# A feed-forward stage with seven forms: x split a second time with the norm's factor in it, and the forms further apart

## The chip, the cores and the metric

The kernel runs on one core of a Trainium2 chip. The core has TensorE (PE in the profile; PEld is its loading of weights), VectorE (DVE), ScalarE (ACT), GpSimd (POOL) and SyncE (SP), which only issues transfers. Each engine takes its own queue of instructions in order; semaphores tie the queues together. The metric is the device time of one execution in microseconds, as the median of several runs.

## The reference

The reference is a decoder trunk of two layers on 256 tokens of 1024 features in float32. Each layer is feed-forward, mixer, feed-forward. All that the change touches is in the feed-forward stages:

```python
def rms_norm(x, g):
    xf = x.astype(jnp.float32)
    y = xf * lax.rsqrt(jnp.mean(xf * xf, axis=-1, keepdims=True) + EPS)
    return (y * g.astype(jnp.float32)).astype(x.dtype)

def swiglu(h, w_gate_up, w_down):
    a, b = jnp.split(h @ w_gate_up, 2, axis=-1)
    return (jax.nn.silu(a) * b) @ w_down

    x = x + 0.5 * swiglu(rms_norm(x, ffn1_norm), ffn1_w_gate_up, ffn1_w_down)
    ...
    x = x + 0.5 * swiglu(rms_norm(x, ffn2_norm), ffn2_w_gate_up, ffn2_w_down)
```

The hidden width is 2816, that is 22 groups of 128 columns for `a` and as many for `b`. The norm multiplies each token by a factor r (one number per token) and each feature by a gain g.

## The kernel before

**Split operands.** Every float32 operand is split into a high part that TensorE reads exactly in its fast float32 form and a low remainder: ScalarE copies (`hi`, L174 or L163), VectorE subtracts (`lo`, L175 or L164). A product is then hi times (hi and lo of x, 512 columns) plus lo times hi of x (256 columns).

**Units.** The weights come in units of 1 MB (128 x 2048). `fetch` loads the next unit of a list (`plan`) from SP's queue into one of four `raw` buffers and splits it in two halves of 128 x 1024 each; the split parts have room for three units (six half tiles each of `hi` and `lo`). `unit` hands the next split unit to TensorE. One unit is fetched ahead of the one in use.

**A feed-forward stage** (`ffn`). x lies with features on the partitions. `split_x` makes the eight tiles of `hx` (high and low part, x times gain g) at the end of the stage before. The upward half makes for each of the 22 groups n a "pair": 32 products over the eight tiles of hx into a bank of PSUM for a and b together. `drain` brings it to the tile `ab` (ScalarE copies one part, L223, VectorE adds the other, L224). `post(n)` follows one pair later: VectorE multiplies `ab` by r (L393), ScalarE takes Silu (L395), VectorE multiplies by b (L396), and `halves` splits the result for the downward half (L246, L247). r itself is made by `sums` during the first two pairs (`factor_spread`, L345 to L360): two products by ones, then five VectorE and ScalarE steps, of which L359 is the last.

**The seven forms.** In three of the four feed-forward stages (all but the very first), four groups, n = 12 to 15, are not made as pairs. Their 512 columns of a and b, for 256 tokens and 1024 features, form a block product of two by two blocks, which is made with seven products of half the size instead of eight (Strassen's and Winograd's scheme). Each form has 16 products into a bank with tokens on the partitions (`by_tokens`, names pa, pe, pg, pf in the trace) and needs a unit of weights of its own: the forms "1", "2" and "4" read parts of hx, the forms "5", "3", "6", "7" read sums of quarters of x (`x_forms`, made from `xg` = x times gain in the buffer `pre`, then split into tiles `sf`). The weights of "1", "5", "6" and "4" lie one after the other in one buffer (`sa`), each made by an accumulating transfer onto the one before (L155, issued by GpSimd, since it adds in flight); "3" and "7" share the buffer `pre` in the same way; "2" has a `raw` buffer. A form's transfer can go out only when the form before it in the same buffer is split. The results are added and subtracted in VectorE (L506 to L514), gated with Silu (`gated`, L471 to L477) and turned back to features by four transposes (`turned`). Since r is a factor per token, and tokens are on the partitions there, `gated` scales by a column of per-token factors, which `factor_tokens` makes with two more small products (st in the trace).

**Banks.** "1" and "2" accumulate in bank a, "5" and "3" in e, "6" has g, "7" is the first in f and "4" writes f again, anew, after "7" was read.

**Order.** TensorE's instructions keep the written order. The other engines' queues are ordered at build time by a planner: of what is ready by its own cost estimates it takes what was written first; `behind` adds an edge that holds one instruction back until another one of the same engine. The written order of the stage is 0, 1, 2, 3, 4, "1", 5, "2", 6, "5", 7, "3", 8, "6", 9, "7", 10, "4", 11, 16, ... 21 (`feed_order`).

Of the kernel before, what the change touches and what calls it, by code (L numbers as in the profile page):

```python
# [18 lines left out]
F32 = mybir.dt.float32  # L19
F32R = mybir.dt.float32r  # L20
# [34 lines left out]
def feed_order():  # L55

    z, forms = [], list(FORMS)
    for n in (*range(GROUP), *range(GROUP + 4, NF)):
        if n >= FIRST and forms:
            z.append(forms.pop(0))  # L60
        z.append(n)
    return z


def feed_units(base):
    return [base + n if isinstance(n, int) else (base, n) for n in feed_order()]

# [5 lines left out]
def trunk_kernel(ctx: ExitStack, tc: tile.TileContext, x_in, w_in, pw_in, qkn_in, rope_in, mask_in, band_in, out):  # L73
# [37 lines left out]
    for base in (0, FU, LU, LU + FU):  # L111
        plan.extend(feed_units(base) if base else range(NF))
# [13 lines left out]
    def fetch(last=None):  # L126

        u = next(plan)
        if isinstance(u, tuple):
            ahead.append(sum_form(*u))  # L130
            return
        raw, hi, lo = buffers()
        n = HALF if u < 4 else 2 * HALF
        for c in range(0, 2 * HALF, n):
            nc.sync.dma_start(raw[:, c:c + n], w_in[u, :, c:c + n])
# [4 lines left out]
        ahead.append((hi, lo))  # L140

    sums_at = {}

    def sum_form(base, f):

        n = base + GROUP
        q = {"11": (n, 0), "12": (n + 2, 0), "21": (n, 1), "22": (n + 2, 1)}
        at, add, src = FORMS[f]
        if at == "c":
            sums_at["c"] = raws.tile([P, 2 * HALF], F32, name="raw", tag="raw")  # L150
        z = sums_at[at].rearrange("p (i c) -> p i c", i=2)
        u, kh = q[src]
        w = w_in[u:u + 2, :, kh * HALF:(kh + 1) * HALF].rearrange("u p c -> p u c")
        if add:
            nc.gpsimd.dma_start(z, w, accum_op=OP.add)  # L155
        else:
            nc.sync.dma_start(z, w)
        _, hi, lo = buffers(False)
        z = z.rearrange("p i (k c) -> p i k c", c=2 * P)
        for h in range(2):  # L160
            a = z[:, :, 2 * h:2 * h + 2, :]
            hv, lv = (t[h].rearrange("p (k i c) -> p i k c", i=2, c=2 * P) for t in (hi, lo))
            act(hv, a, AF.Copy)  # L163
            tt(lv, a, hv.bitcast(F32), op=OP.subtract)  # L164
        return hi, lo

    def buffers(raw=True):
        raw = raws.tile([P, 2 * HALF], F32, name="raw", tag="raw") if raw else None
        hi = [parts.tile([P, HALF], F32R, name="hi", tag="hi") for _ in range(2)]
        lo = [parts.tile([P, HALF], F32R, name="lo", tag="lo") for _ in range(2)]  # L170
        return raw, hi, lo

# [160 lines left out]

    def factor_tokens():

        st = quarter("st")[:, 0, :2]
        for t in range(2):
            mm(st[:, t:t + 1], lhsT=acc[:, t * P:(t + 1) * P], rhs=ones[:, :1], start=True, stop=True)
        rt = small.tile([P, 2], F32, name="rt", tag="rt", bufs=2)
        rsqrt(rt, st, 1.0 / D)  # L340
        nt = small.tile([P, 2], F32, name="nt", tag="nt", bufs=1)
        nc.vector.tensor_scalar(nt, rt, -1.0, None, op0=OP.mult)
        return rt, nt

    def factor_spread():  # L345
# [19 lines left out]
    def ffn(after, n0=0, end=False, col=None):  # L365
        gs, gt = [], []

        def room(n, m):
            g = acts.tile([P, m, 2, S], F32R, name=n, tag=n)
            gt.append(g)  # L370
            gs.extend(g[:, i] for i in range(m))

        room("ga", 8)
        room("gc", 4)
        abs_ = {}

# [9 lines left out]
        def sums():  # L386
            r.append(factor_spread())
            if not n0:
                r.append(factor_tokens())

        def post(n):
            ab = abs_[n]
            scaled = tt(ab, ab, bc2(r[0]), op=OP.mult)  # L393
            sg = small.tile([P, S], F32, name="sg", tag="sg", bufs=2)
            act(sg, ab[:, 0, :], AF.Silu)  # L395
            tt(sg, sg, ab[:, 1, :], op=OP.mult)  # L396
            halves(gs[n], sg)
            return scaled

        if n0:  # L400
            room("gd", 4)
            room("gb", NF - 16)
            ws = [unit() for _ in range(n0)]
# [14 lines left out]
        else:  # L418
# [7 lines left out]
            drain(wide(1), pss[1])  # L426

            sums_at["a"] = acts.tile([P, 2 * HALF], F32, name="sa", tag="gd")
            pre = acts.tile([P, 12 * S], F32, name="pre", tag="gb")
            sums_at["b"] = pre[:, :NK * S]  # L430
            xg = pre[:, :NK * S].rearrange("p (k s) -> p k s", s=S)
            vt = acts.tile([P, 2, GW], F32, name="vt", tag="v")
# [3 lines left out]
            sf = {}  # L436

            def x_forms():

                late = drained[-1]  # L440
                for k in range(NK):
                    behind(act(xg[:, k, :], x[:, k, :], AF.Copy, scale=gain[:, l_of[0], col + k:col + k + 1]), late)  # L442
                a11, a21 = (xg[:, :4, t * P:(t + 1) * P] for t in range(2))
                a12, a22 = (xg[:, 4:, t * P:(t + 1) * P] for t in range(2))
# [26 lines left out]
            def gated(c, t, n, sign):  # L471

                c = c.rearrange("p (i j s) -> p i j s", i=2, j=2)
                sc = r[1][sign][:, t:t + 1]
                sg = small.tile([P, S], F32, name="sg", tag="sg", bufs=2)
                act(by_half(sg), c[:, :, 0, :], AF.Silu, scale=sc)
                stt(by_half(gq[2 * t + n]), c[:, :, 1, :], sc, by_half(sg), op0=OP.mult, op1=OP.mult)  # L477

            def turned(n):

                pt = quarter("pt")
                for i in range(2):
                    for t in range(2):
                        keep(nc.tensor.transpose(pt[:, i, t * P:(t + 1) * P], gq[2 * t + n][:, i * P:(i + 1) * P], ident))
                g = gt[2][:, 2 * n:2 + 2 * n]
                act(g[:, :, 0, :], pt, AF.Copy)
                tt(g[:, :, 1, :], pt, g[:, :, 0, :].bitcast(F32), op=OP.subtract)
# [3 lines left out]
            def strassen(f):  # L491
# [9 lines left out]
                elif f == "2":  # L501
                    gated(z, 0, 0, 0)
                elif f == "5":
                    act(p5, z, AF.Copy)
                elif f == "6":
                    tt(p1, z, p1, op=OP.add)  # L506
                    tt(c12, bank["e"], p1, op=OP.add)
                    gated(c12, 0, 1, 1)
                elif f == "7":
                    tt(p5, z, p5, op=OP.add)  # L510
                    tt(p5, p5, p1, op=OP.add)
                    gated(p5, 1, 1, 1)
                elif f == "4":
                    tt(p1, z, p1, op=OP.add)  # L514
                    gated(p1, 1, 0, 0)

            late = []
            wait = [0, 1]
            for i, n in enumerate(feed_order()[2:]):
                if isinstance(n, str):  # L520
                    strassen(n)
                    if n in "74":
                        late.append([2, 1 if n == "7" else 0])
                    continue
                pair(unit(), wide(n))
                fetch()
                if i == 0:
# [4 lines left out]
                if n == GROUP - 1:  # L532
                    room("gd", 4)
                    room("gb", NF - 16)
                for z in late:
# [3 lines left out]
            for m in wait:  # L539
                post(m)  # L540
        for b in range(NK * NF):
# [476 lines left out]
```

## Time and profile before

| what | value |
|---|---|
| three runs | 1009.3, 1012.51, 1013.52 us |
| median | 1012.51 us |
| the profiled execution | 1010.54 us, its span 1008.8 us |
| TensorE busy | 997.2 us |
| VectorE busy | 808.9 us |
| ScalarE busy | 641.5 us |
| mean granted clock of TensorE | 0.998 of full |

The span is the time from the first to the last instruction of the program; the time of an execution has a little around it. A row of the time line gives start, duration, engine, line, operation, out<-in, shapes, and in brackets the idle time of the engine before it with what ended it. Consecutive instructions of one engine overlap by a little, so the distance between starts tells what one costs in a full queue.

### The profile page before, as it was taken

To read this page: it belongs to the slowest core of one execution; us is meant where nothing else is said; L and a number is where in the kernel's file an instruction comes from. 1 tells how busy PE (TensorE), PEld (TensorE's weight loads), DVE (VectorE), ACT (ScalarE), POOL (GpSimd) and SP (SyncE) were. 2 spreads that over 40 slices of the span, in tenths; PEclk is the share of its full clock that TensorE was granted. 3 is DMA by queue.
4 is the path that set the end of the run, shared out by engine and by line. 5 is a ranking of instruction groups with operands and counts; after the bars stand their busy time and mean duration, and the time that the engine had idled before them with its cause. 6 is when DMAs were issued, how large, how long until landed. Compare 5 with 4: busy or idle time off the path is not lost.

```text
span 1008.8 us, 16140 instructions
## 1 busy us (share of the span) xinstructions
PE 997.2 (99%) x6336; PEld 904.4 (90%) x6336; DVE 808.9 (80%) x1217; ACT 641.5 (64%) x1026; POOL 30.6 (3%) x58
## 2 busy tenths in 40 slices
PE   9999999999999999999999999999999999999998
PEld 8988988898899988889998888988989999889888
DVE  6998866698978897986679798666988888889852
ACT  7866655657756876665578576555677568666641
POOL 0000000002000010000000000000020000000000
PEclk9999999999999999999999999999999999999999
DMA  8855655644537488565558856555544464967540
GB/s 301 309 203 209 209 195 187 213 167 150 188 136 262 162 243 238 201 215 183 195 209 235 229 204 229 193 204 183 184 182 173 142 245 161 261 195 250 205 151 21
DMA packets 34156, 202.34 MB, mean 201 GB/s; under 512 B 3488, under 2 KB 4768, under 8 KB 13088
## 3 DMA queue, kind: packets, MB, share of 16 engines
q1 hardware_dynamic: 30816, 188.74, 52.6%
q0 software_dynamic: 3264, 12.58, 6.8%
q8 instruction: 49, 0.80, 0.3%
q14 instruction: 27, 0.22, 0.1%
HBM read 200.26 MB, written 1.05 MB: 200 GB/s over the span
## 4 chain that ended last, share of the span: by engine, by line
PE 81%; DMA 9%; DVE 4%; ACT 3%; issue 2%; SPq 0%; ACTq 0%; POOLq 0%
PE ps L103 65%; DMA sa<-w 7%; PE pt L103 7%; PE two L103 4%; DVE lo L164 1%; DMA pre<-w 1%; PE pe L103 1%; DVE lo L175 1%; PE pf L103 1%; PE sc L103 1%; ACT hi L163 1%; ACT pre L442 1%; PE pt L657 1%; DVE ab L224 1%; PE y L103 1%
## 5 line engine op out<-in xcount | busy, mean ns | idle before, releaser
L103 PE MATMUL ps<-hx,hi 128*128 128x512 f32 x1504 | 506.9, 384 | 0.9 <-ACT hi L174 0.9
L175 DVE TENSOR_TENSOR lo<-raw,hi 128x1024 fp32r<-128x1024 f32 (+2 forms) x348 | 411.1, 1189 | 111.5 <-ACT hi L174 109.2
L174 ACT ACTIVATE hi<-raw 128x1024 fp32r<-128x1024 f32 (+2 forms) x348 | 352.8, 1026 | 180.0 <-PE ps L103 128.5
L103 PE MATMUL ps<-hx,lo 128*128 128x256 f32 x1504 | 411.0, 273 | 0.0
L103 PEld LDWEIGHTS ps<-hx,hi 128*128 128x128 f32 x1504 | 282.4, 188 | 51.8 <-ACT hi L174 1.2
L103 PEld LDWEIGHTS ps<-hx,lo 128*128 128x128 f32 x1504 | 282.6, 188 | 0.3 <-DVE lo L175 0.3
L103 PE MATMUL ps<-ga,hi 128*128 128x512 f32 (+1 forms) x264 | 87.0, 376 | 0.0
L103 PE MATMUL ps<-ga,lo 128*128 128x256 f32 x256 | 69.9, 273 | 0.0
L103 PE MATMUL ps<-gb,hi 128*128 128x512 f32 (+1 forms) x198 | 65.6, 376 | 0.0
L103 PE MATMUL pt<-hi,hx 128*128 128x512 f32 x192 | 65.1, 385 | 0.0
L103 PEld LDWEIGHTS ps<-ga,hi 128*128 128x128 f32 x264 | 49.0, 188 | 8.3
L103 PE MATMUL pt<-lo,hx 128*128 128x256 f32 x192 | 52.6, 274 | 0.0
L393 DVE TENSOR_TENSOR ab<-ab,r 128x512 f32<-128x512 f32 x76 | 51.9, 685 | 0.9
L103 PE MATMUL ps<-gb,lo 128*128 128x256 f32 x192 | 52.4, 273 | 0.0
L224 DVE TENSOR_TENSOR ab<-ps,ab 128x512 f32<-128x512 f32 x74 | 50.6, 684 | 0.9
L395 ACT ACTIVATE sg<-ab 128x256 f32<-128x256 f32 x76 | 31.3, 415 | 30.4 <-DVE ab L393 29.3
L103 PEld LDWEIGHTS ps<-ga,lo 128*128 128x128 f32 x256 | 48.1, 188 | 0.0
L163 ACT ACTIVATE hi<-sa 128x1024 fp32r<-128x1024 f32 x24 | 25.3, 1052 | 30.3 <-DMA sa<-w 26.9
L103 PE MATMUL ps<-gc,hi 128*128 128x512 f32 (+1 forms) x132 | 44.3, 376 | 0.0
L103 PE MATMUL ps<-gd,hi 128*128 128x512 f32 (+1 forms) x132 | 44.3, 376 | 0.0
L103 PE MATMUL ps<-mk,hi 128*128 128x256 f32 x256 | 44.1, 275 | 0.0
L223 ACT ACTIVATE ab<-ps 128x512 f32<-128x512 f32 x74 | 42.9, 579 | 0.0
(215 smaller groups left out, 1463.9 us busy)
## 6 DMA issues: line engine op xcount, KB each, us to landing
raw<-w SPq DMA_DIRECT2D x167, 1024.0 KB, 4.9
sa<-w POOLq DMA_DIRECT2D x9, 1024.0 KB, 10.0
raw<-w SPq DMA_DIRECT2D x16, 256.0 KB, 5.3
sa<-w SPq DMA_DIRECT2D x3, 1024.0 KB, 5.8
pre<-w SPq DMA_DIRECT2D x3, 1024.0 KB, 5.1
pre<-w POOLq DMA_DIRECT2D x3, 1024.0 KB, 13.0
out_dram<-gx SPq DMA_DIRECT2D x8, 128.0 KB, 2.6
gx<-x SPq DMA_DIRECT2D x3, 256.0 KB, 5.4
```

What stands on the lines that cost most here:

```text
L103: return keep(nc.tensor.matmul(*args, **kw))
L163: act(hv, a, AF.Copy)
L164: tt(lv, a, hv.bitcast(F32), op=OP.subtract)
L174: act(hi, w, AF.Copy)
L175: return tt(lo, w, hi.bitcast(F32), op=OP.subtract)
L223: act(t, ps[:, :, 1, :], AF.Copy)
L224: drained.append(tt(t, ps[:, :, 0, :], t, op=OP.add))
L393: scaled = tt(ab, ab, bc2(r[0]), op=OP.mult)
L395: act(sg, ab[:, 0, :], AF.Silu)
L442: behind(act(xg[:, k, :], x[:, k, :], AF.Copy, scale=gain[:, l_of[0], col + k:col + k + 1]), late)
L657: keep(nc.tensor.transpose(pt[:, h, o * P:(o + 1) * P], pr[:, h, c * P:(c + 1) * P], ident))
```

## The change

Five things change, all in the three stages with forms, beside a tidier `buffers`:

1. After pair 2, `scaled_x` makes `xs` = x times gain times r, eight steps of VectorE (128 x 256), where `xg` was made without r by eight ScalarE copies. After pair 3, `split_again` splits `xs` into `hx` once more, over the old values: four ScalarE copies and four VectorE subtractions of 128 x 512. All pairs from 4 on, and all forms, then have r in their products.
2. So `post` multiplies by r only for the groups 0 to 3, `gated` scales by 1 or -1, and `factor_tokens` goes.
3. `x_forms` moves from behind pair 2 to behind pair 4, its first sums held back until pair 4 is drained.
4. The order is written out: 0 to 5, "1", 6, "2", 7, "5", 8, "3", 9, 10, "7", 11, 16, "6", 17, 18, "4", 19, 20, 21. "7" comes before "6"; the sums for the last quarter move from "7" to "6" accordingly, and both `turned` come after "4".
5. The first loads of the two buffers ("1" and "3") are issued by GpSimd instead of SP.

```diff
-FIRST = 5
+FEED = (0, 1, 2, 3, 4, 5, "1", 6, "2", 7, "5", 8, "3", 9, 10, "7", 11, 16, "6", 17, 18, "4", 19, 20, 21)
...
         if add:
             nc.gpsimd.dma_start(z, w, accum_op=OP.add)
+        elif at == "c":
+            nc.sync.dma_start(z, w)
         else:
-            nc.sync.dma_start(z, w)
+            nc.gpsimd.dma_start(z, w)
...
         def sums():
             r.append(factor_spread())
-            if not n0:
-                r.append(factor_tokens())
...
-        def post(n):
+        def post(n, scale=True):
             ab = abs_[n]
-            scaled = tt(ab, ab, bc2(r[0]), op=OP.mult)
+            scaled = tt(ab, ab, bc2(r[0]), op=OP.mult) if scale else None
...
+            def scaled_x():
+
+                for k in range(NK):
+                    c = gain[:, l_of[0], col + k:col + k + 1]
+                    stt(xs[:, k, :], x[:, k, :], c, r[0], op0=OP.mult, op1=OP.mult)
+
+            def split_again():
+
+                for k in range(0, NK, 2):
+                    act(hx[:, k:k + 2, 0, :], xs[:, k:k + 2, :], AF.Copy)
+                    tt(hx[:, k:k + 2, 1, :], xs[:, k:k + 2, :], hx[:, k:k + 2, 0, :].bitcast(F32), op=OP.subtract)
...
             def x_forms():
 
-                late = drained[-1]
-                for k in range(NK):
-                    behind(act(xg[:, k, :], x[:, k, :], AF.Copy, scale=gain[:, l_of[0], col + k:col + k + 1]), late)
...
-                tt(s1, a22, a21, op=OP.subtract)
+                behind(tt(s1, a22, a21, op=OP.subtract), last)
+                behind(tt(s3, a11, a21, op=OP.subtract), last)
                 stt(s2, s1, -1.0, a11, op0=OP.mult, op1=OP.subtract)
-                tt(s3, a11, a21, op=OP.subtract)
...
                 elif f == "6":
                     tt(p1, z, p1, op=OP.add)
+                    tt(p5, p5, p1, op=OP.add)
+                    gated(p5, 1, 1, -1.0)
                     tt(c12, bank["e"], p1, op=OP.add)
-                    gated(c12, 0, 1, 1)
+                    gated(c12, 0, 1, -1.0)
                 elif f == "7":
                     tt(p5, z, p5, op=OP.add)
-                    tt(p5, p5, p1, op=OP.add)
-                    gated(p5, 1, 1, 1)
...
-            for i, n in enumerate(feed_order()[2:]):
+            for i, n in enumerate(FEED[2:]):
                 if isinstance(n, str):
                     strassen(n)
-                    if n in "74":
-                        late.append([2, 1 if n == "7" else 0])
+                    if n == "4":
+                        late += [[1, 1], [2, 0]]
                     continue
                 pair(unit(), wide(n))
                 fetch()
-                if i == 0:
+                if n == 2:
+                    scaled_x()
+                if n == 3:
+                    split_again()
+                if n == 4:
                     x_forms()
                 for m in wait[:2]:
-                    post(m)
+                    post(m, m < 4)
...
             for m in wait:
-                post(m)
+                post(m, False)
```

More of the change, by code (lines that the diff above doesn't have):

```diff
@@ L52 @@
 }
[L55 to L66, printed above, removed]
 C_G1, C_GM, C_G2, C_BG, C_PS, NG = 0, 8, 16, 24, 40, 44
@@ L111, in trunk_kernel @@
     for base in (0, FU, LU, LU + FU):
-        plan.extend(feed_units(base) if base else range(NF))
+        plan.extend([base + n if isinstance(n, int) else (base, n) for n in FEED] if base else range(NF))
         plan.extend(range(base + NF, base + NF + NF // 2))
@@ L132, in fetch @@
         raw, hi, lo = buffers()
-        n = HALF if u < 4 else 2 * HALF
-        for c in range(0, 2 * HALF, n):
-            nc.sync.dma_start(raw[:, c:c + n], w_in[u, :, c:c + n])
+        nc.sync.dma_start(raw, w_in[u])
         for h in range(2):
@@ L140, in fetch, with buffers, part_buffers @@
         ahead.append((hi, lo))
+    def buffers():
+        raw = raws.tile([P, 2 * HALF], F32, name="raw", tag="raw")
+        return raw, *part_buffers()
+    def part_buffers():
+        return [[parts.tile([P, HALF], F32R, name=n, tag=n) for _ in range(2)] for n in ("hi", "lo")]
     sums_at = {}
@@ L165, in sum_form @@
         return hi, lo
[L167 to L171, printed above, removed]
     def split(w, hi, lo):
@@ L332, in spread @@
         return r
[L334 to L343, printed above, removed]
     def factor_spread():
@@ L365, in ffn, with room @@
     def ffn(after, n0=0, end=False, col=None):
[L366 to L374, printed above, removed]
+        gs, gt = {}, {}
+        def room(name, n0, m):
+            g = acts.tile([P, m, 2, S], F32R, name=name, tag=name)
+            gt[name] = g
+            gs.update({n0 + i: g[:, i] for i in range(m)})
+        room("ga", 0, 8)
+        room("gc", 8, 4)
         abs_ = {}
@@ L400, in ffn @@
         if n0:
-            room("gd", 4)
-            room("gb", NF - 16)
+            room("gd", 12, 4)
+            room("gb", 16, NF - 16)
             ws = [unit() for _ in range(n0)]
@@ L426, in ffn @@
             drain(wide(1), pss[1])
+            pre = acts.tile([P, 12 * S], F32, name="pre", tag="gb")
             sums_at["a"] = acts.tile([P, 2 * HALF], F32, name="sa", tag="gd")
-            pre = acts.tile([P, 12 * S], F32, name="pre", tag="gb")
             sums_at["b"] = pre[:, :NK * S]
-            xg = pre[:, :NK * S].rearrange("p (k s) -> p k s", s=S)
+            xs = pre[:, :NK * S].rearrange("p (k s) -> p k s", s=S)
             vt = acts.tile([P, 2, GW], F32, name="vt", tag="v")
@@ L436, in ffn @@
             sf = {}
-            def x_forms():
-                late = drained[-1]
-                for k in range(NK):
-                    behind(act(xg[:, k, :], x[:, k, :], AF.Copy, scale=gain[:, l_of[0], col + k:col + k + 1]), late)
-                a11, a21 = (xg[:, :4, t * P:(t + 1) * P] for t in range(2))
-                a12, a22 = (xg[:, 4:, t * P:(t + 1) * P] for t in range(2))
+            def scaled_x():
[6 more added lines that the diff above has]
+                    tt(hx[:, k:k + 2, 1, :], xs[:, k:k + 2, :], hx[:, k:k + 2, 0, :].bitcast(F32), op=OP.subtract)
+            def x_forms():
+                last = drained[-1]
+                a11, a21 = (xs[:, :4, t * P:(t + 1) * P] for t in range(2))
+                a12, a22 = (xs[:, 4:, t * P:(t + 1) * P] for t in range(2))
                 s1, s2 = (pre[:, (8 + 2 * i) * S:(10 + 2 * i) * S].rearrange("p (k s) -> p k s", s=P) for i in range(2))
                 s3, s4 = (vt[:, i, :].rearrange("p (k s) -> p k s", s=P) for i in range(2))
-                tt(s1, a22, a21, op=OP.subtract)
+                behind(tt(s1, a22, a21, op=OP.subtract), last)
+                behind(tt(s3, a11, a21, op=OP.subtract), last)
                 stt(s2, s1, -1.0, a11, op0=OP.mult, op1=OP.subtract)
-                tt(s3, a11, a21, op=OP.subtract)
                 stt(s4, s2, -1.0, a12, op0=OP.mult, op1=OP.subtract)
@@ L473, in gated @@
                 c = c.rearrange("p (i j s) -> p i j s", i=2, j=2)
-                sc = r[1][sign][:, t:t + 1]
                 sg = small.tile([P, S], F32, name="sg", tag="sg", bufs=2)
-                act(by_half(sg), c[:, :, 0, :], AF.Silu, scale=sc)
-                stt(by_half(gq[2 * t + n]), c[:, :, 1, :], sc, by_half(sg), op0=OP.mult, op1=OP.mult)
+                act(by_half(sg), c[:, :, 0, :], AF.Silu, scale=sign)
+                stt(by_half(gq[2 * t + n]), c[:, :, 1, :], sign, by_half(sg), op0=OP.mult, op1=OP.mult)
             def turned(n):
@@ L484, in turned @@
                         keep(nc.tensor.transpose(pt[:, i, t * P:(t + 1) * P], gq[2 * t + n][:, i * P:(i + 1) * P], ident))
-                g = gt[2][:, 2 * n:2 + 2 * n]
+                g = gt["gd"][:, 2 * n:2 * n + 2]
                 act(g[:, :, 0, :], pt, AF.Copy)
@@ L501, in strassen @@
                 elif f == "2":
-                    gated(z, 0, 0, 0)
+                    gated(z, 0, 0, 1.0)
                 elif f == "5":
@@ L506, in strassen @@
                     tt(p1, z, p1, op=OP.add)
+                    tt(p5, p5, p1, op=OP.add)
+                    gated(p5, 1, 1, -1.0)
                     tt(c12, bank["e"], p1, op=OP.add)
-                    gated(c12, 0, 1, 1)
+                    gated(c12, 0, 1, -1.0)
                 elif f == "7":
                     tt(p5, z, p5, op=OP.add)
-                    tt(p5, p5, p1, op=OP.add)
-                    gated(p5, 1, 1, 1)
+                    room("gb", 16, NF - 16)
                 elif f == "4":
                     tt(p1, z, p1, op=OP.add)
-                    gated(p1, 1, 0, 0)
+                    gated(p1, 1, 0, 1.0)
+                    room("gd", 12, 4)
             late = []
             wait = [0, 1]
-            for i, n in enumerate(feed_order()[2:]):
+            for i, n in enumerate(FEED[2:]):
                 if isinstance(n, str):
                     strassen(n)
-                    if n in "74":
-                        late.append([2, 1 if n == "7" else 0])
+                    if n == "4":
+                        late += [[1, 1], [2, 0]]
                     continue
@@ L539, in ffn @@
             for m in wait:
-                post(m)
+                post(m, False)
+        gs = [gs[n] for n in range(NF)]
         for b in range(NK * NF):
```

5 lines of the change are left out of this document (1 added, 4 removed).

## The prediction

> **What bounds the kernel now.** I read the page's busy line first, then who TensorE waits for, then the chain of waits.
>
> ```profile
> span 1008.8 us, 16140 instructions
> PE 997.2 (99%) x6336; PEld 904.4 (90%) x6336; DVE 808.9 (80%) x1217; ACT 641.5 (64%) x1026; POOL 30.6 (3%) x58
> ```
>
> TensorE works in 99% of the span, so only its own work, its few pauses and its clock can move the time. Next, TensorE's waits (total us, times, longest):
>
> ```profile
> PE pf L103 <- DVE tk L510: 6.2, 3, 2.4
> ```
>
> One place in each of the three stages with the seven forms makes nearly all of it: form "4" starts late. The chain of waits (start, us, what) shows how:
>
> ```profile
> 404.12 0.61 DVE tk L510
> 404.87 4.57 PE pf L103 x16
> ...
> 415.35 5.33 PE ps L103 x32
> ...
> 514.68 0.34 PE st L103 x4
> ...
> 584.16 2.92 PE pf L103 x16
> ...
> 905.27 2.90 PE pf L103 x16
> ```
>
> Form "4" writes the PSUM bank that form "7" has just used. VectorE adds that bank into p5 (L510) only at 404.12, because other work stood ahead in its queue. An undisturbed pair takes 5.33. The first "4" takes 4.57 where the other two take 2.92 and 2.90, though it is the same work; the clock says why (us, busy times, granted clock as PEclk):
>
> ```profile
> 340.00:355.00 15.00, 15.00 (x92) 13.46 (x91) 13.81 (x28) 14.48 (x27) 1.09 (x1) 1.00 0.43 141
> 355.00:370.00 15.00, 15.00 (x91) 13.46 (x90) 13.52 (x18) 10.76 (x16) 0.57 (x2) 1.00 0.93 277
> 404.00:409.00 5.00, 4.13 (x15) 3.59 (x16) 5.00 (x9) 2.73 (x6) 0.00 (x0) 0.66 0.20 31
> 584.00:587.00 3.00, 2.84 (x17) 2.59 (x18) 3.00 (x5) 1.69 (x4) 0.00 (x0) 1.00 0.00 0
> ```
>
> After the longest pause (2.4) the granted clock is 0.66 over 404 to 409; after a shorter one at 584 it stays 1.00. So a wait of about 2.4 here costs a further 4.57 - 2.91 = 1.66. The Trainium skill (TensorE: Matmul & The Clock Gate, "What's actually happening") puts the fall to half clock after an idle window of about 3.4 us. The trace differs: it fell after 2.4, so the row decides; by the page the 1.66 would not belong to the pause and the sum would come out 1.7 us less favourable. The first two rows matter below: VectorE is busy 13.81 and 13.52 of 15 where the forms begin. It is the engine that is nearly full.
>
> **What the change takes away.** (1) The second user of bank "f" moves off the first. Now "7", pair 10, "4" follow each other; afterwards pairs 11 and 16, form "6", pairs 17 and 18 lie between "7" and "4", over 20 us at 5.33 a pair. What was late, the addition into p5, is then early by far: 6.2 gone in the three stages, and the 1.66 of slow clock with it. (2) The token factors go: two small products in each of the three stages (the row "PE st x4", 0.34), 3 x 0.34 = 1.0, straight off TensorE. Their small VectorE and ScalarE steps go too and count as nothing, since TensorE did not wait for them. Together -6.2 - 1.7 - 1.0 = **-8.9**. TensorE keeps every other product, so this is also the most there is.
>
> ```profile
> L393 DVE TENSOR_TENSOR ab<-ab,r 128x512 f32<-128x512 f32 x76 | 51.9, 685 | 0.9
> ```
>
> (3) 14 of the 18 groups of such a stage lose their multiplication by r (L393), 42 of the 76. That is VectorE time, worth something only where VectorE is late. The first four keep it.
>
> **What it adds, and where.** Rows of VectorE and of TensorE in the first such stage:
>
> ```profile
> 340.01 0.42 DVE L359 SCALAR_TENSOR_TENSOR r<-a,r 128x256 f32<-128x256 f32 x1
> ...
> 353.11 0.68 DVE L454 TENSOR_TENSOR sf<-pre,sf 128x512 fp32r<-128x512 f32 x1
> 353.71 0.42 DVE L247 TENSOR_TENSOR ga<-sg,ga 128x256 fp32r<-128x256 f32 x1
> 354.04 0.68 DVE L454 TENSOR_TENSOR sf<-vt,sf 128x512 fp32r<-128x512 f32 x1
> 354.65 0.68 DVE L393 TENSOR_TENSOR ab<-ab,r 128x512 f32<-128x512 f32 x1
> 355.25 1.22 DVE L175 TENSOR_TENSOR lo<-raw,hi 128x1024 fp32r<-128x1024 f32 x1
> 356.39 0.68 DVE L224 TENSOR_TENSOR ab<-ps,ab 128x512 f32<-128x512 f32 x1
> ...
> 369.04 0.48 DVE L477 SCALAR_TENSOR_TENSOR vt<-pa,rt,sg 128x256 f32<-128x256 f32 x1
> 369.43 0.68 DVE L393 TENSOR_TENSOR ab<-ab,r 128x512 f32<-128x512 f32 x1
> ```
>
> ```profile
> 353.69 0.39 PE L103 MATMUL pa<-hi,hx 128*128 128x512 f32 x1
> 356.43 0.39 PE L103 MATMUL ps<-hx,hi 128*128 128x512 f32 x1
> 369.88 0.39 PE L103 MATMUL pe<-hi,sf 128*128 128x512 f32 x1
> ```
>
> I price a VectorE step by the distance to the next start: 0.60 for 512 columns (354.65 to 355.25), 1.14 for half a weight unit (355.25 to 356.39), 0.33 for 256 columns (353.71 to 354.04), 0.39 for the two-operand step with a column of scalars (369.04 to 369.43). A form takes 2.74 (353.69 to 356.43). I leave TensorE's times of before in place: pair 4 starts at 353.69 - 5.33 = 348.4, pair 5 at 353.7, form "1" now after it at 359.0. r is there at about 340.35.
>
> *Second split, and pair 4 behind it.* `scaled_x` is eight steps of 0.39 = 3.1, `split_again` four ScalarE copies and four VectorE subtractions of 0.60 = 2.4. Pair 4 is the first to read the new hx, and TensorE takes its instructions in order, so everything behind pair 4 waits with it. Ahead of the first subtraction in written order stand: drain of pair 1 0.60, `scaled_x` 3.12, the posts of 0 and 1 at 0.60 + 0.33 + 0.33 = 1.26 each, drain of pair 2 0.60; with its own 0.60 it is done at 340.35 + 7.44 = 347.8, 0.6 before pair 4. hx is overwritten in place, but quarter by quarter behind pair 3's reading, and pair 4 uses a quarter in a fourth of 5.33 = 1.33 against 0.60 to make one. Bounds 0 to 0.6 (half a weight unit of 1.14 slipped in before it); I take 0.
>
> *Form "1".* This is the place that I expect to pay. Ahead of the second half of its weights in VectorE's queue stand, from r on: drains 1 to 4 (2.40), `scaled_x` 3.12, posts 0 to 3 with their scaling (5.04), `split_again` 2.40, the weights of pair 5 (2 x 1.14 = 2.28), `x_forms` with four sums and four subtractions (8 x 0.60 = 4.80), and its own 2.28: 22.3. There are 340.35 to 359.0 + 1.37 = 360.4 for it, 20.05. So 2.3 is missing. `x_forms` is needed only by form "5", but it is written ahead of the weights of "1", so it goes first. Bounds: 0, if the planner lets enough of `x_forms` fall behind (its last four subtractions alone are 2.4), to 2.3 + 1.2 = 3.5, with the idle time that VectorE had between 340 and 355 even now (15.00 - 13.81). I take 1.6: the two last steps of post 3 (0.66) wait for ScalarE anyway and may fall behind. 3 x 1.6 = **+4.8**. From "1" on to "5" VectorE has two forms and two pairs, 16.1 us, for 12.0 of work (two drains 1.2, two posts without scaling 1.3, four weight units 9.1, one `gated` 0.4), so it does not pile up.
>
> *The accumulating transfers and the order 7 before 6.* Rows of the transfers (issue to landing, and the stages of form "7"):
>
> ```profile
> pre<-w SPq DMA_DIRECT2D x3, 1024.0 KB, 5.1
> pre<-w POOLq DMA_DIRECT2D x3, 1024.0 KB, 13.0
> ```
>
> ```profile
> 353.91 8.95 DMA sa<-w
> ```
>
> ```profile
> 389.40 1.06 ACT L163 ACTIVATE hi<-pre 128x1024 fp32r<-128x1024 f32 x1 [2.09 <-DMA pre<-w]
> ```
>
> ```profile
> 376.46 1.20 POOL L155 DMA_DIRECT2D pre<-w  x1 [5.58 <-DVE lo L164]
> ```
>
> Form "7" adds into the buffer of "3" once "3" is split. Now the transfer goes out at 376.46, 6.6 after form "5" began (369.88); with 13.0 to landing and 1.06 for the copy and 1.14 for the subtraction, with the way between them about 2.4, its first half is ready 22.0 after "5" began. Afterwards "5", 8, "3", 9, 10 give 2 x 2.74 + 3 x 5.33 = 21.5: 0.5 late if nothing else changed. But the transfer of "6" no longer runs across its beginning nor that of "4" across its end; alone, such a transfer took 8.95. Bounds 0 to 0.5 each; I take 0. The loads of "1" and "3" leave SP's queue, past nothing but their own chain on POOL, and SP has only raw weights left behind; no cost. The Trainium skill (DMA: Bandwidth & Descriptors, "SWDGE vs HWDGE vs iDMA") lets plain transfers go from SP or ScalarE and only accumulating ones from GpSimd, which speaks against that move. The rows agree in direction (5.1 from SP, 8.95 at best from POOL).
>
> **Sum.** -8.9 + 4.8 = -4.1. The profiled execution took 1010.5 (span 1008.8), so 1006.4 of its kind; the median of the three runs is 1012.5, 2.0 above it, which gives **1008.4**.
>
> **Rivals.** *Nothing new waits.* The planner fills VectorE's gaps with the weights of "1" early. For it: VectorE did idle 1.2 between 340 and 355 and 1.5 after. Against: the 22.3. Time 1012.5 - 8.9 = 1003.6.
>
> *VectorE is too full and the clock falls with it (slower).* At form "1" the whole 3.5 is paid and each pause costs 1.66 of clock, as the one at 404 did: 3 x (3.5 + 1.66) = 15.5, less 8.9, +6.6: 1019.1. It turns slower from 3.0 a stage without the clock, or from 1.3 with it. For it: VectorE is at 92% there and gets 5.5 more before its savings begin at group 4. Against: of the three pauses now, only the one of 2.4 cost clock; the other two, (6.2 - 2.4) / 2 = 1.9 each, did not.
>
> *Form "7" is late by its chain.* If "3", loaded by POOL after `x_forms` has read xs (about 361), takes 13.0, it lands at 374, where pair 7 frees room for its split from about 372.5: 1.5 late, with the 0.5 above 2.0 in each stage: -4.1 + 6 = +1.9, 1014.4. Against: alone a transfer took 8.95.
>
> That "4" still waits for "7" I leave out: 20 us lie between.
>
> **How the numbers follow.** The forecast has 0.48, no new wait 0.27, the full VectorE 0.13, the late "7" 0.12. The likeliest's own range is 1006 to 1011 (its 1.6 moved by 0.8 each way). The range of 1002.5 to 1015.5 reaches from the first rival less 1 to the third plus 1. About 0.5%, 5.1 us, is what a measurement of this kernel can tell from no change. Faster by more: all of no new wait and 0.18 of the forecast, 0.45. Slower: 0.10 of the full VectorE, 0.03 of the late "7", 0.01 of the forecast, 0.14. The rest, 0.41, is the same.
>
> **What would show it.** TensorE's wait for L510's successor and the "st" products are gone; the scaling of ab counts 76 - 42 = 34 instead of 76; the clock is 1.00 at "4". In place of it stands a wait of "pa" for VectorE's subtraction of the weights of "1", 1 to 2 us, three times. A wait of "ps" for hx at pair 4 would show my order on VectorE wrong; a wait of the first "pf" for the split of "pre" the third rival. No new wait of TensorE at all, or a clock below 1.00 near "1", makes the prediction wrong.

## The result and the profile after

The changed kernel takes 1025.55 us (median of four runs, 1024.96 to 1026.81) against 1013.01 for the kernel before on the same chip: a ratio of 1.0132, with a 95% interval of 1.0103 to 1.016. (A ratio here and below is an estimate from the runs together, so it is not exactly the quotient of the two medians.) It is slower, and outside the predicted range. The profiled execution has a span of 1025.0 where the one before had 1008.8: 16.2 more.

The busy lines of the page of the changed kernel, and its group for the scaling by r:

```profile
span 1025.0 us, 16029 instructions
PE 1001.9 (98%) x6324; PEld 903.0 (88%) x6324; DVE 796.3 (78%) x1196; ACT 636.8 (62%) x1011; POOL 35.0 (3%) x64
...
L367 DVE TENSOR_TENSOR ab<-ab,r 128x512 f32<-128x512 f32 x34 | 23.0, 688 | 0.4
```

What the change removes is removed: 12 fewer records of products, 34 scalings instead of 76, 12.6 us less work on VectorE. Yet the span grew by more than TensorE's busy time did. So TensorE waits. Its waits (total us, times, longest):

```profile
PE ps L89 <- DVE ab L211: 10.3, 5, 2.7
PE pf L89 <- ACT hi L156: 3.0, 3, 1.5
PE pf L89 <- DVE lo L157: 2.3, 3, 0.8
PE ps L89 <- DVE lo L162: 1.5, 6, 0.3
```

The old wait for the addition into p5 is not there. There are two new ones. "pf" waits for the split of form "7"'s weights (L156 and L157), in every stage. And "ps", a pair, waits for L211, the VectorE half of a drain: its PSUM bank was not emptied. Who held these two engines up stands in their own waits, ScalarE's first:

```profile
ACT hi L156 <- DMA pre<-w: 36.0, 3, 12.4
ACT hi L156 <- DMA sa<-w: 18.9, 6, 6.3
```

ScalarE stands still 12 us in each stage until the weights of "7" (tile `pre`) have landed. The time lines of ScalarE, VectorE and GpSimd in the first such stage show how that reaches TensorE:

```profile
385.39 0.58 ACT L210 ACTIVATE ab<-ps 128x512 f32<-128x512 f32 x1
398.05 2.00 ACT L156 ACTIVATE hi<-pre 128x1024 fp32r<-128x1024 f32 x2 [12.07 <-DMA pre<-w]
...
403.14 0.58 ACT L210 ACTIVATE ab<-ps 128x512 f32<-128x512 f32 x1
...
425.80 2.01 ACT L156 ACTIVATE hi<-sa 128x1024 fp32r<-128x1024 f32 x2 [6.34 <-DMA sa<-w]
```

```profile
399.13 2.36 DVE L157 TENSOR_TENSOR lo<-pre,hi 128x1024 fp32r<-128x1024 f32 x2 [11.79 <-ACT hi L156]
...
404.40 0.68 DVE L211 TENSOR_TENSOR ab<-ps,ab 128x512 f32<-128x512 f32 x1
```

```profile
374.93 1.19 POOL L146 DMA_DIRECT2D sa<-w  x1 [13.60 <-DVE sg L370]
380.74 1.18 POOL L146 DMA_DIRECT2D pre<-w  x1 [4.62 <-ACT tk L487]
413.78 1.19 POOL L146 DMA_DIRECT2D sa<-w  x1 [31.86 <-ACT ab L210]
```

Read them together. GpSimd issues the transfer of "6" (sa) at 374.93, because its buffer comes free first, and that of "7" (pre) at 380.74, although "7" is now used before "6". ScalarE's queue has the split of "7" right behind the drain of pair 8 (385.39), ahead of the drains of pairs 9 and 10, which are written before it; so nothing behind it runs until the transfer lands at 398; VectorE stands still for 11.79 as well. Pair 9 ends meanwhile, but its drain comes at 403.14 and 404.40. So "7" starts late, and pair 11, which needs pair 9's bank, waits until 404.40 is done. The split of "6" stood in the same line, so the transfer of "4", onto the same buffer, goes out only at 413.78, and 425.80 is the same thing once more: pair 19 waits 2.71 for a late drain. The chain of waits has it as one path:

```profile
380.74 17.20 DMA pre<-w
398.05 1.06 ACT hi L156
...
404.40 0.69 DVE ab L211
405.14 6.75 PE ps L89 x39
...
413.78 11.92 DMA sa<-w
```

**Where the time is, unit by unit.** The distance from the first product of a unit to that of the next, read from TensorE's time line, in us, for the three stages in order. The wait for a unit's weights is counted to the unit before it, so "7" here holds its own inner waits and the wait of pair 11.

| unit | undisturbed | before | after | six_transfer_held | six_first | six_first_one_split |
|---|---|---|---|---|---|---|
| pair behind "1" | 5.35 | 5.35, 5.34, 5.34 | 6.44, 6.42, 6.44 | 6.38, 6.42, 6.27 | 6.40, 6.38, 6.04 | 5.35, 5.35, 5.35 |
| pairs 9 and 10 | 10.69 | | 12.14, 12.36, 11.58 | 10.69, 10.68, 10.96 | 10.69, 10.69, 10.69 | 10.68, 10.69, 10.69 |
| "7" | 2.75 | 2.75, 2.75, 2.75 | 5.99, 5.99, 5.99 | 2.75, 2.75, 2.68 | 2.75, 2.75, 2.75 | 2.75, 2.75, 2.75 |
| pairs 11 and 16 | 10.69 | | 10.78, 12.43, 10.79 | 10.69, 10.69, 10.96 | 10.69, 10.68, 10.69 | 10.69, 10.69, 10.69 |
| "4" | 2.75 | 4.41, 2.76, 2.74 | 5.62, 2.96, 4.50 | 3.72, 3.84, 2.68 | 2.75, 2.75, 2.75 | 2.75, 2.75, 2.75 |
| from the products for r to the downward half, three stages together | | 335.2 | 351.9 | 333.4 | 329.7 | 327.6 |

(In the two kernels with "6" first, the rows "9 and 10" and "11 and 16" are the pairs ahead of "6" and ahead of "7". In the kernel before, the wait ahead of "4" is counted to pair 10, which takes 7.95, 7.29 and 7.45 instead of 5.35.) Above the undisturbed times stand, in the changed kernel, 3.3 behind "1", 4.0 ahead of "7", 9.7 in and behind it, 1.9 in pairs 11 and 16 (nearly all of it slow clock in the second stage), 4.8 behind "4": 23.7. With the predicted 8.9 taken away that is +14.8 of the 16.2. Of the 1.4 left over, 0.8 is at the token products, whose removal brought 0.2 net and not 1.0, since pair 4 took most of it back (below); the rest lies in small pieces that I did not follow.

### The profile page after: what moved, and what is told of

It reads as the page before. It is cut to its first block, busy times and chain, and to the rows that moved or that the text cites. A ratio compares the mean times of both kernels' runs of the same rounds, so it can differ in the third digit from the quotient of the medians.

```text
span 1025.0 us, 16029 instructions
## 1 busy us (share of the span) xinstructions
PE 1001.9 (98%) x6324; PEld 903.0 (88%) x6324; DVE 796.3 (78%) x1196; ACT 636.8 (62%) x1011; POOL 35.0 (3%) x64
## 4 chain that ended last, share of the span: by engine, by line
PE 75%; DVE 11%; DMA 9%; ACT 2%; issue 2%; SPq 0%; ACTq 0%; POOLq 0%
PE ps L89 59%; PE pt L89 6%; DMA pre<-w 5%; PE two L89 4%; DMA sa<-w 3%; DVE lo L162 2%; PE pe L89 2%; DVE lo L157 2%; DVE ab L211 1%; DVE pre L416 1%; PE sc L89 1%; PE pa L89 1%; DVE sg L370 1%; DVE ab L367 1%; DVE hx L422 1%
## 5 line engine op out<-in xcount | busy, mean ns | idle before, releaser
L89 PE MATMUL ps<-hx,hi 128*128 128x512 f32 x1504 | 511.6, 386 | 11.9 <-DVE ab L211 10.3
L211 DVE TENSOR_TENSOR ab<-ps,ab 128x512 f32<-128x512 f32 x74 | 50.8, 686 | 0.9
L157 DVE TENSOR_TENSOR lo<-sa,hi 128x1024 fp32r<-128x1024 f32 x24 | 29.2, 1218 | 16.8 <-ACT hi L156 16.8
L89 PEld LDWEIGHTS ps<-gb,hi 128*128 128x128 f32 x198 | 36.7, 188 | 6.2
## 6 DMA issues: line engine op xcount, KB each, us to landing
pre<-w POOLq DMA_DIRECT2D x6, 1024.0 KB, 12.6
```

Of the source, the lines that this page charges most:

```text
L89: return keep(nc.tensor.matmul(*args, **kw))
L211: drained.append(tt(t, ps[:, :, 0, :], t, op=OP.add))
```

## The experiments

Two theories stood against each other. **A:** the transfer of "7" stands in line behind that of "6", and what waits for it blocks the engines. **B:** the second split fills VectorE, and that sets the time. Each ratio is against the kernel before on the same chip.

| run | what | median us | kernel before | ratio (95%) |
|---|---|---|---|---|
| six_transfer_held | changed kernel, transfer of "6" behind that of "7" | 1007.4 | 1009.63 | 0.9971 (0.9953 to 0.999) |
| six_first | changed kernel, form "6" before "7" | 1005.23 | 1009.63 | 0.9953 (0.9932 to 0.9973) |
| order_alone | new order, no second split | 1032.31 | 1009.63 | 1.0212 (1.0183 to 1.0241) |
| own_bank | kernel before, "4" in a bank of its own | 1009.76 | 1009.63 | 0.999 (0.9975 to 1.0006) |
| six_first_one_split | new order with "6" before "7", no second split | 1002.52 | 1011.64 | 0.992 (0.9897 to 0.9942) |
| six_first_sp_loads | six_first, "1" and "3" loaded from SP | 1006.6 | 1011.64 | 0.9952 (0.9937 to 0.9968) |
| second_split_alone | old order, second split | 1023.84 | 1011.64 | 1.013 (1.0108 to 1.0151) |
| six_first_late_sums | six_first, two sums split later | 1008.27 | 1011.64 | 0.9973 (0.9958 to 0.9988) |
| seven_split_held | changed kernel, split of "7" behind the drain of pair 10 | 1018.63 | 1009.66 | 1.0106 (1.0075 to 1.0137) |

**1. Only the order of two transfers.** Everything else is the changed kernel.

```diff
         if add:
-            nc.gpsimd.dma_start(z, w, accum_op=OP.add)
+            sent[f] = nc.gpsimd.dma_start(z, w, accum_op=OP.add)
+            if f == "6":
+                behind(sent[f], sent["7"])
```

> The changed kernel, with one edge more: GpSimd issues the transfer of form 6 only behind that of form 7. Theory A (the transfer of 7 stands in line behind that of 6, ScalarE and VectorE wait for it with the drains of pairs 9 and 10 behind them): 7's transfer takes 9 to 11 us instead of 17.2, ScalarE's wait of 12 shrinks below 4, TensorE's waits at form 7 and at pair 11 go; about 5 us less in each of three stages, 1009 to 1013 in all. Theory B (VectorE is too full because of the second split): no change, 1024 to 1027.

Measured: 0.9971, from slower to a little faster. The chain of waits of this kernel has the transfer of "7" as

```profile
382.56 10.27 DMA pre<-w
...
408.65 12.07 DMA sa<-w
```

This whole execution lies 1.8 later than that of the changed kernel (the transfer of "5" goes out at 359.04 against 357.23), so the transfer of "7" goes out at the same moment of the stage (382.56 against 380.74) and lands 6.9 earlier in it, since nothing stands ahead of it. Now "6" stands behind it, issued 0.74 later, and pays instead (the number at the end is us from issue to landing):

```profile
pre<-w POOLq DMA_DIRECT2D x1, 1024.0 KB, 10.3
sa<-w POOLq DMA_DIRECT2D x1, 1024.0 KB, 19.1
```

The first of the two is not slowed by the second and the second takes nearly twice as long: they land one after the other, and do not share the time evenly. "6" is used late enough to bear it. "7" and pair 11 then wait for nothing (2.75 in the table). ScalarE still waits for `pre`, 5.3 at most, which hurts nobody. What is left is the same fault at "4", smaller: TensorE's waits

```profile
PE ps L89 <- DVE ab L214: 1.7, 2, 0.9
```

Theory A is shown: this one edge is worth the whole loss. VectorE's work is unchanged, so B falls as the cause of it.

**2. The other order of use.** The transfers stay as they go out; the forms follow them.

```diff
-FEED = (..., 9, 10, "7", 11, 16, "6", 17, 18, "4", 19, 20, 21)
+FEED = (..., 9, 10, "6", 11, 16, "7", 17, 18, "4", 19, 20, 21)
...
                 elif f == "6":
                     tt(p1, z, p1, op=OP.add)
-                    tt(p5, p5, p1, op=OP.add)
-                    gated(p5, 1, 1, -1.0)
...
                 elif f == "7":
                     tt(p5, z, p5, op=OP.add)
+                    tt(p5, p5, p1, op=OP.add)
+                    gated(p5, 1, 1, -1.0)
```

> The changed kernel with 6 before 7 again (3, 9, 10, 6, 11, 16, 7, 17, 18, 4, the last sum of the fourth quarter back behind 7), so the forms are used in the order in which their transfers go out. Theory A: 6 lands before it is used and 7 has 13 us more; no long wait at either; 1005 to 1012. Theory B: as the changed kernel, 1022 to 1027.

Measured: 0.9953. GpSimd's time line of this kernel:

```profile
374.91 1.19 POOL L146 DMA_DIRECT2D sa<-w  x1 [13.60 <-DVE sg L370]
380.72 1.18 POOL L146 DMA_DIRECT2D pre<-w  x1 [4.62 <-ACT tk L487]
390.31 1.19 POOL L146 DMA_DIRECT2D sa<-w  x1 [8.41 <-DVE lo L157]
```

"6" and "7" go out at the same moments as in the changed kernel, within 0.02. Only now "6" is used first, so its buffer is free early and "4" goes out at 390.31 instead of 413.78. The transfer of "7" is slow here too, 15.42 from issue to landing, but it has two pairs and a form more until it is needed. All waits at forms are gone, at "4" too, and the two runs agree: it was the order of the two forms against the order of their transfers.

**3. The two halves of the change apart.** `order_alone` is the changed kernel with `scaled_x` and `split_again` taken out, `x_forms` back behind pair 2 with its ScalarE copies, `post` scaling every group and the token factors back. `second_split_alone` is the kernel before with the second split and all that goes with it, in the old order and with its loads on SP.

```diff
 (order_alone, against the changed kernel)
                 if n == 2:
-                    scaled_x()
-                if n == 3:
-                    split_again()
-                if n == 4:
                     x_forms()
                 for m in wait[:2]:
-                    post(m, m < 4)
+                    post(m)
```

> The changed order of pairs and forms with the loads from GpSimd, but without the second split: x times gain by ScalarE after pair 2, r by post for every group, the token factors in gated, as in the kernel before. Theory A: the same line of transfers, the same waits at form 7; 1020 to 1028. Theory B: VectorE has its early time back, 1004 to 1008.

```diff
 (second_split_alone, against the kernel before)
-                if i == 0:
+                if n == 2:
+                    scaled_x()
+                if n == 3:
+                    split_again()
+                if n == 4:
                     x_forms()
                 for m in wait[:2]:
-                    post(m)
+                    post(m, m < 4)
```

> The second split in the old order of forms with the loads from SP. If VectorE has no room for it ahead of form 1, which stands right behind pair 4 there: waits of 2 to 4 us in each stage on top of the kernel before, 1014 to 1022 where the kernel before takes 1010. If the split is hidden and the late addition at form 4 is all that is left: 1006 to 1011.

Measured: 1.0212 and 1.013. Each half alone makes the kernel slower. In both the mean granted clock is lower, 0.992 and 0.990 against 0.998 in the kernel before and in the changed kernel. Worked out from these shares of their spans (an estimate), they lost the worth of some 8 and 10 us of full clock, the other two 2 each; so part of these two losses is slow clock behind the waits. `order_alone` has the same waits as the changed kernel, without any second split ("7" is 6.59 three times, its transfer took 14.24 in the first stage). In sum they are no longer than those of the changed kernel, so the lower clock is what the trace shows for its being slower still; why the clock fell more often here no run shows.

```profile
PE ps L89 <- DVE ab L211: 10.0, 7, 2.6
PE pf L89 <- ACT hi L156: 3.3, 3, 1.6
```

`second_split_alone` waits elsewhere: form "2" (the second "pa") for its weights.

```profile
PE pa L89 <- DVE lo L155: 11.3, 3, 4.3
PE ps L89 <- DVE lo L160: 2.0, 3, 0.9
```

Its ScalarE and VectorE there, in the first stage:

```profile
363.31 1.06 ACT L154 ACTIVATE hi<-sa 128x1024 fp32r<-128x1024 f32 x1 [4.51 <-DMA sa<-w]
364.27 0.61 ACT L435 ACTIVATE sf<-vt 128x512 fp32r<-128x512 f32 x1
```

```profile
364.91 0.69 DVE L436 TENSOR_TENSOR sf<-vt,sf 128x512 fp32r<-128x512 f32 x1 [3.51 <-ACT sf L435]
365.52 1.22 DVE L155 TENSOR_TENSOR lo<-raw,hi 128x1024 fp32r<-128x1024 f32 x1
```

ScalarE's split of "5" waits 4.51 for its transfer; a copy of a sum stands behind it; VectorE's part of that sum waits 3.51 for the copy; and behind that stands the second half of the weights of "2". It is the same kind of chain as at "7": work that is ready, in line behind work that waits for a transfer. So the second split has a cost of its own in the old order, but not by VectorE being too full: it stood idle (11.49 busy of the 15.00 from 355 to 370). This chain is read from the rows; no run takes it apart.

**4. What each half is worth once "6" comes first.** `six_first_one_split` is `order_alone` with the edit of experiment 2.

> The order with 6 before 7 and without the second split (r by post, token factors, x times gain by ScalarE). If the order is what frees the stage and the second split is worth little by itself: within 3 us of the run with both, 1003 to 1009, the 1.1 of waiting at pair 6 gone and 0.36 of token products back in each stage. If the 14 scalings less per stage are what keeps VectorE on time: waits for drains come back, 1012 to 1020.

Measured: 0.992, the fastest of all here, and faster than both kernels. `six_first_sp_loads`, which has the second split and ran on the same chip, has 0.9952: the medians are 4.1 us apart, and the intervals of the ratios overlap by 0.0005, but every run of the one (1004.81 at most) lies below every run of the other (1005.08 at least). The table says where most of it is: with the second split the pair behind "1" takes 6.04 to 6.40 (in six_first), without it 5.35, 2.8 in the three stages. The token products that the second split removes save nothing here: from the products for r to "1" six_first takes 24.56, 24.63 and 25.08, and six_first_one_split, which keeps them, 24.67 three times. So in this order the second split very probably costs time; it saves none.

**5. Loads from SP.**

```diff
-        elif at == "c":
-            nc.sync.dma_start(z, w)
         else:
-            nc.gpsimd.dma_start(z, w)
+            nc.sync.dma_start(z, w)
```

> The order with 6 before 7 and the second split, with the first loads of 1 and 3 issued from SP's queue as before. If these two loads are off the chain: same as from GpSimd, 1003 to 1007. If the line of transfers on GpSimd is what is short: 2 to 5 us less. If SP's raw weights get stuck behind the load that waits for x: 2 to 8 us more.

Measured: 0.9952 against 0.9953 for six_first. Which engine issues the two plain loads makes no difference that shows.

**6. Two sums split later.** To relieve VectorE behind "1", the splits for "3" and "6" are written behind pair 6 instead of behind pair 4.

```diff
+                if n == 6:
+                    split_forms(*later)
```

> The order with 6 before 7, with the splits of x's sums for forms 3 and 6 written behind pair 6 instead of behind pair 4. If the 1.1 that TensorE waits at pair 6 in each stage is VectorE doing these two splits too early: the waits go, 1001 to 1003.5 against 1005. If VectorE is simply full until form 5, the wait moves to the next pair or form: 1004 to 1007.

Measured: 0.9973, no better than six_first. The pair behind "1" became longer (7.14, 7.14, 7.04), and TensorE's wait grew:

```profile
PE ps L89 <- DVE lo L162: 4.2, 3, 1.4
```

Where these splits are written does not relieve the place; the idea failed, and I did not follow why the queue came out worse.

**7. A bank of its own for "4", in the old order.** In the kernel before, "4" adds onto the sum of "7" in bank f (the words "anew" in the description above are wrong there), so a bank of its own needs one VectorE addition more.

```diff
-                b = {..., "7": "f", "4": "f"}[f]
+                b = {..., "7": "f", "4": "h"}[f]
...
                 elif f == "4":
+                    tt(p1, bank["f"], p1, op=OP.add)
                     tt(p1, z, p1, op=OP.add)
```

> The kernel before with one thing changed: form 4 writes a PSUM bank of its own, and VectorE adds the bank of 7 into p1 in one addition more. If the late addition out of bank f alone held form 4 up, the 6.2 of waiting and the 1.7 of slow clock go: 1004.5 to 1007 against 1013 before. If form 4's weights, split at 402.39 where TensorE came at 402.27, are the next to be late, part of it comes back: 1007 to 1011.

Measured: 0.999, no change. The wait of 6.2 for the bank is gone, and in its place stands

```profile
PE ps L103 <- DVE ab L224: 5.9, 4, 1.7
```

a pair that waits for a late drain. The addition that this edit puts in takes VectorE about 0.6 in a stage (the price of 512 columns in the prediction), less than a third of the new wait. So the bank alone was not the cause; VectorE was late at that place, and whoever asks it next waits.

**8. The blocked drains apart from the late weights.** The ScalarE copy of the weights of "7" may not pass the drain of pair 10. (The edge goes to the VectorE half of that drain: `behind` can also tie an instruction to one of another engine, which its description above leaves out.)

```diff
-            act(hv, a, AF.Copy)
+            hi_part = act(hv, a, AF.Copy)
+            if f == "7":
+                behind(hi_part, drained[-1])
```

> The changed kernel, with one edge more: ScalarE's copy of form 7's weights stands behind the drain of pair 10 in its queue, the transfers as they are. If most of the loss is that the drains of pairs 9 and 10 stand behind a copy that waits 12 us for its transfer: ScalarE's wait there falls below 2, TensorE's wait for the drain at pair 11 goes, form 7 itself still starts 1 to 2 late; 1014 to 1020 in all. If the late form is the loss and the drains only wait along with it: 1023 to 1027, as the changed kernel.

Measured: 1.0106, whose interval overlaps that of the changed kernel (1.0103 to 1.016). TensorE's waits:

```profile
PE pf L89 <- ACT hi L156: 4.9, 3, 1.6
PE pf L89 <- DVE lo L159: 2.3, 3, 0.8
...
PE ps L89 <- DVE ab L213: 0.4, 1, 0.4
```

The waits for drains fell from 10.3 to 0.4, and those of "7" for its weights stayed (7.2 after 5.3), since its transfer takes as long as before (16.76 in the first stage). So both are there, the late weights and the drains that were locked up behind them. How much each is worth in time this run doesn't settle: the two kernels ran on different chips, and by the medians the changed kernel loses 12.5 against the kernel before on its chip, this one 9.0; the intervals of the ratios overlap.

## Why the prediction was wrong

**The step that failed** is "The accumulating transfers and the order 7 before 6", where I took 0 out of bounds of 0 to 0.5 each. Its reason was that "the transfer of "6" no longer runs across its beginning". It ran ahead of it: a form's transfer goes out when its buffer is free, and "5" leaves its buffer before "3" does, whatever the written order of "6" and "7". I had the rows for that (the "5" of before in front of "3"), and I costed the transfer of "7" as if it were alone. Behind that of "6" it took 17.20, alone 10.27 (experiment 1), and even in the kernel before 13.0. The Trainium skill (DMA: Bandwidth & Descriptors, "SWDGE vs HWDGE vs iDMA") says that GpSimd's way of issuing has only one queue allocated; 17.20 against 10.27 agrees with that, and I had not weighed it.

My bounds failed for a second reason: they counted only how late "7" itself would be, a fraction of 1 us. The larger part of TensorE's new waiting, 10.3 beside 5.3 for the weights of "7", came from what stood behind the splits of "7" and "4" in the queues of ScalarE and VectorE; its share of the lost time stays open (experiment 8). I had asked that question of VectorE at "1", and not of the instruction that waits for a transfer.

**Taken away, -8.9.** Right in the place, in the order with "6" first. The wait of 6.2 and the slow clock at "4" went, in both kernels with "6" first: "4" takes 2.75 three times. From the kernel before to `six_first_one_split` the three upward halves lost 7.6 (335.2 to 327.6: 8.5 around "4", less 0.9 that one pair behind "2" waits anew), where 6.2 + 1.7 = 7.9 was worked out. In the changed kernel itself a slow clock came back (below). Experiment 7 adds what I had not seen: it is the distance between the forms that helps, not the bank. The -1.0 for the token products hardly arrived: from the first products for r to form "1" it is 24.56, 24.62 and 24.58 in the changed kernel and 24.67 three times in order_alone, which keeps them, 0.2 in all. The next point has taken the rest.

**Pair 4, taken as 0 (0 to 0.6).** A little was paid. The groups by line have the weight loads of the pairs as one (the idle time of the engine, by what ended it, stands at the end):

```profile
L89 PEld LDWEIGHTS ps<-hx,hi 128*128 128x128 f32 x1504 | 283.0, 188 | 67.0 <-DVE ab L211 12.4 <-ACT hi L161 1.6 <-DVE hx L422 1.1
```

1.1 of waiting for the new hx, 0.4 a stage, inside the bounds; by the starts of the products the pairs up to "1" became 0.8 longer in the three stages.

**Form "1", 3 x 1.6 = 4.8.** The mechanism was right, the place and the size a little off. VectorE is full there: in windows of 15 us (PE, PEld, DVE, ACT, POOL) it has no gap,

```profile
340.00:355.00 15.00, 14.96 (x89) 13.22 (x89) 15.00 (x28) 12.43 (x20) 0.00 (x0) 1.00 0.28 87
355.00:370.00 15.00, 14.50 (x84) 12.43 (x84) 15.00 (x23) 12.32 (x21) 1.95 (x2) 1.00 0.85 253
```

where it had 13.81 and 13.52 before. But the planner put the weights of "1" ahead of `x_forms`, the case for which I had named the bound 0, and the backlog came out one unit later, at the pair behind "1": 1.1 in each stage, 3.3 for 4.8.

```profile
361.53 0.39 PE L89 MATMUL ps<-hx,hi 128*128 128x512 f32 x1
362.14 0.38 PE L89 MATMUL ps<-hx,lo 128*128 128x256 f32 x1 [0.22 <-DVE lo L162]
```

I had said that it would not pile up from "1" on; it did by one pair.

**The loads of "1" and "3" from GpSimd, no cost.** Right (experiment 5). The rule of the Trainium skill that I had set against it (DMA: Bandwidth & Descriptors, "SWDGE vs HWDGE vs iDMA") makes no time here: 0.9952 by SP, 0.9953 by GpSimd.

**The sum.** -4.1 is what comes out where the failed term is really 0: experiment 1 measured 0.9971, that is -2.9, and experiment 2 0.9953, that is -4.7. That they lie so near is in part luck. By the distances from products for r to the downward half, six_first has -8.5 around "4", +2.8 behind "1" and +0.2 up to "1", -5.5 in all: the saving of the token products was priced 1.2 too high and the cost at "1" 2.0 too high, and the two partly cancel.

**The rivals.** "Form "7" is late by its chain" named the right place and the sign that it would show, the first "pf" waiting for the split of "pre". Its cause, a late load of "3", was wrong (that load took 7.89, 8.50 and 8.18, not 13.0), and its price of 2.0 a stage was that of "7" alone: in the table the changed kernel pays (4.0 + 9.7) / 3 = 4.6 a stage at "7" and 4.8 in all at "4" afterwards. "VectorE is too full and the clock falls with it" had 1019.1, nearer to the time than any other, but by a cause that the runs exclude: experiment 1 leaves VectorE as full, and is not slower. The argument against the late "7" went by a transfer that took 8.95 alone, and the prediction called that the best of GpSimd's; the second stage of the kernel before has one of 8.44. Either way that row didn't apply: that transfer was alone, and "7" was not.

## What to carry to other kernels

Where two uses are exchanged, look at what lets their transfers go out: here they kept the order in which their buffers came free, and one issued behind another landed late by about what was left of that one. An instruction that waits for a transfer should be priced with everything behind it in its engine's queue, the drains above all: here it locked two engines for 12 us in a kernel whose busiest engine has no slack. A wait that is removed at one place (a bank) comes back at the next one if the engine behind it is still late, so ask whether the work or only the place was late.

## What the hardware showed that I had not expected

**Transfers from one issuer.** A 1 MB accumulating transfer from GpSimd took 10.27 with none of GpSimd's ahead of it (from 8.44 to 13.38 in the kernels before, after and six_transfer_held), 14.24 and 17.20 when issued 6 behind another, 19.06 when issued 0.74 behind. In the changed kernel and in six_transfer_held the second of two landed 8.8 to 9.9 after the first, in all six stages. Plain loads do not show it as clearly: in the changed kernel that of "3", issued 3.35 behind the transfer of "5", landed only 2.49 after it. Loads from SP ran beside them, so that the figures are not those of an otherwise idle core; the same issue times are harmless when the uses come in that order (experiment 2).

**The clock.** I had priced a fall to 0.66 by the length of a pause, 2.4 us. Three pauses of the changed kernel show more. Those of 2.00 and 2.71 ahead of pairs 11 and 19 of the first stage left the clock at 1.00, and one of 1.96 in the second stage was followed by a slow stretch. TensorE's rows at the three pauses, then the windows behind them in order (the clock is the third number from the end, ahead of DMA share and GB/s):

```profile
405.14 0.49 PE L89 MATMUL ps<-hx,hi 128*128 128x512 f32 x1 [2.00 <-DVE ab L211]
...
434.98 0.50 PE L89 MATMUL ps<-hx,hi 128*128 128x512 f32 x1 [2.71 <-DVE ab L211]
...
589.97 0.50 PE L89 MATMUL ps<-hx,hi 128*128 128x512 f32 x1 [1.96 <-DVE ab L211]
```

```profile
405.00:410.00 5.00, 4.86 (x29) 4.39 (x30) 4.20 (x8) 3.83 (x7) 0.00 (x0) 1.00 0.62 210
435.00:440.00 5.00, 5.00 (x29) 4.43 (x30) 4.20 (x7) 3.62 (x6) 0.00 (x0) 1.00 0.61 210
590.00:595.00 5.00, 5.00 (x20) 4.32 (x21) 4.20 (x7) 3.95 (x7) 0.00 (x0) 0.66 0.62 210
```

So the length of a pause alone doesn't decide. The Trainium skill (TensorE: Matmul & The Clock Gate, "What's actually happening") says that the activity is watched in windows that run on by themselves, so that it matters where in a window a pause falls; these three rows agree with that, and not with a threshold on the pause. The idle window of the same section, against which the prediction set the pause of 2.4, is not borne out by the pause of 1.96 either, though that one and the one of 2.00 have shorter waits at "7" some us ahead of them. No run here shows the windows themselves.
